# The last output row of a Strassen product made in two halves of 128 tokens

## The chip, the cores and the metric

The kernel runs on one core of one Trainium2 chip. The metric is device microseconds for one execution, the median of several. The profile is one execution taken by the hardware profiler; its own time stands beside its span below.

## The reference

One block of a streaming encoder on 512 tokens with 1024 channels: two parallel mixers (RWKV-7 and RG-LRU), cross-attention, a gated ConvFFN, and a last RMSNorm. What matters here is its end:

```python
def conv_ffn(h, w_in, conv_w, conv_b, w_out):
    u = h @ w_in
    gate = causal_dwconv(u[..., :D_FF], conv_w, conv_b)
    return (jax.nn.gelu(gate) * u[..., D_FF:]) @ w_out
...
x = x + conv_ffn(rms_norm(x, norm_ffn_g[l]), w_ffn_in[l], ffn_conv_w[l],
                 ffn_conv_b[l], w_ffn_out[l])
return rms_norm(x, norm_final_g)
```

`w_ffn_out` is 2816 x 1024. The last RMSNorm needs, for each token, the sum of squares over all 1024 channels, so no token can be stored before all its channels are there.

## The kernel before

Channels lie on the 128 partitions, in 8 blocks (`KB`), tokens along the free dimension (`T` = 512). The product with `w_ffn_out` is a Strassen product on a 2 x 2 split: channels out in two halves of 4 blocks (`MQ`), tokens in two halves of 256 (`H`, columns 0 to 255 and 256 to 511), the inner dimension in two halves of 11 blocks (`HB`). It takes seven products, called A11, A12, s1, s2, s3, A22 and s4 in that order, each 4 rows `m` of 11 weight blocks `k` of 128x128. Their sums build up in PSUM tiles, `X` (named ox_ps) and `YZ` (oyz_ps). The last product, s4, adds into `YZ[m][:, H:T]`, so when row m of it is done, tokens 256 to 511 of channel block m are final.

`out_product` (L1347) makes one product: for each (m, k) of `out_order` (L1313) it takes a weight tile from the stream `uf`, and `mm3` (L165 to L168) issues three matmuls, since a factor is kept as a high and a low part, both of type F32R (fp32r in the rows of ACT and DVE; the matmul rows write f32 for both types): high x high (L166), high x low (L167), low x high (L168). Each loads its own 128x128 weights (the PEld rows) and streams 256 columns. The weights come by `out_weights` (L1315): 8 tiles to a load on SP's queue, a cast on ACT (L1340) and a subtraction on DVE (L1341), three buffers deep.

When a row is done, `done(m)` is called. For s4 that is `c12` (L1422). It calls `ffn_out` (L1373): DVE adds the PSUM tile into the residual `xr` (L1380), ACT squares it (L1382), the block is scaled by the norm's weight (L1386 on ACT, or L1384 on DVE for the last row), and DVE adds the square to the running sum `sso` (L1388). For the last row, m = 3, `c12` goes over the two halves of 128 tokens, and for each calls `ffn_out` and then `final` (L1391):

- PE sums over the partitions with a matrix of ones: `sso` (L1394) and the last square (L1395), both plain F32 tiles, 128 columns to a half
- ACT takes Ln (L1406) and then twice Exp, once into PSUM for DVE (L1407) and once into SBUF for GpSimd (L1408)
- the 8 channel blocks are multiplied: two by GpSimd, twice three by DVE (all L1411), and stored as each is ready: DVE's first three from ACT's queue (L1415), the other two pieces from SP's queue (L1413)

Tokens 0 to 255 were normed and stored by `c21` after product A22, before this. The kernel is written with a Tile scheduler, which orders each engine's instructions by their place in the program unless a priority or an explicit order says otherwise, and puts in the waits between engines. `tc.issue_after` lets what is written inside follow a given instruction in the order.

Of the kernel before, what the change touches and what calls it, by code (L numbers as in the profile page):

```python
# [12 lines left out]
ALU = mybir.AluOpType  # L13
# [4 lines left out]
P = 128  # L18
T = 512
D = 1024  # L20
KB = D // P
# [37 lines left out]
def hybrid_block_kernel(ctx: ExitStack, tc: tile.TileContext, xT_d, mT_d, pv_d, cst_d, win_d, wk_d, wv_d,  # L59
# [18 lines left out]
    def rw_ps(name, pool=None, tag="rw", **kw):  # L78
        return (pool or prw).tile([P, T], F32, tag=tag, name=name, **kw)
# [9 lines left out]
    def par(name, i, n=1):  # L89
        o = PV[name][0]  # L90
        return pv[:, o + i:o + i + n]
# [45 lines left out]
    class Units:  # L137
# [10 lines left out]
        def next(self):  # L148
            if self.left == 0:
                self.fill()  # L150
            i = self.i
            self.i += 1
            self.left -= 1
            return self.hi[:, i * P:(i + 1) * P], self.lo[:, i * P:(i + 1) * P]
# [10 lines left out]
    def mm3(ps, lh, ll, rh, rl, start, stop, **kw):  # L165
        first = PE.matmul(ps, lh, rh, start=start, stop=False, **kw)  # L166
        PE.matmul(ps, lh, rl, start=False, stop=False, **kw)  # L167
        PE.matmul(ps, ll, rh, start=False, stop=stop, **kw)  # L168
        return first
# [3 lines left out]
    def sum_behind(ins, n=1):  # L173

        for put in islice(sums, n):
            tc.add_manual_dep(tc.keep_in_program_order(put()).ins, ins.ins.name, mybir.DependencyInfo(
                mybir.DependencyClass.Sync, mybir.DependencyReason.DATA), reason="pace of the sums")
# [44 lines left out]
    def rsqrt(out, src, scale, bias, load=True):  # L222

        if load:
            ins = ln_exp_set()
            with tc.issue_after(ins.ins):
                S.activation(out, src, AF.Ln, scale=scale, bias=bias)
                S.activation(out, out, AF.Exp, scale=-0.5)
        else:
            S.activation(out, src, AF.Ln, scale=scale, bias=bias)  # L230
            S.activation(out, out, AF.Exp, scale=-0.5)
# [51 lines left out]
    with tc.tile_pool(name="p0", bufs=1, reuse_waits="tile") as p0:  # L283
# [6 lines left out]
        o = PV["nmem"][0]  # L290
# [96 lines left out]
        for hf in range(2):  # L387
            pss = [(mm_ps if hf else rw_ps)(f"v_ps{hf}_{i}") for i in range(2)]
            for k2 in range(4):
                wh, wl = next(st)  # L390
# [105 lines left out]
    HB = FB // 2  # L496
    MQ = KB // 2
# [240 lines left out]
    with tc.tile_pool(name="pz", bufs=1, reuse_waits="tile") as pz:  # L738
# [9 lines left out]
        for s in range(30, -1, -1):  # L748
            n = 31 - s
# [25 lines left out]
    for i0 in (0, 16):  # L775
# [3 lines left out]
        for i in range(16):  # L779
            for e in range(2):  # L780
                r, k = rows[0][e], rows[1][e]
                PE.matmul(psh[e][k, i * 32:(i + 1) * 32], BZ[r, i0 + i, 32:64], ZA[r, i0 + i, :],
                          start=True, stop=True)
        for e, copy in enumerate((S.copy, V.tensor_copy)):
            k = rows[1][e]
            copy(Hs[e][k], psh[e][k].rearrange("p (i t) -> p i t", t=32))
        for i in range(16):
            for e in range(2):
                r, k = rows[0][e], rows[1][e]
                PE.matmul(pso[e][r, i * 32:(i + 1) * 32], Hs[e][k, i, :], BZ[k, i0 + i, 32:64],  # L790
                          start=True, stop=True)
# [357 lines left out]
    H = T // 2  # L1149
# [19 lines left out]
    for m in order:  # L1169
# [5 lines left out]
        i = m % 4  # L1175
# [17 lines left out]
        else:  # L1193
            sq = ph.tile([P, T], F32, tag="rsq", name=f"rsq_nffn{m}")
# [33 lines left out]
    gsets = [[pc.tile([P, n, 2, H], F32R, name=f"go0_{n}", bufs=1) for n in (8, 3)], [None, None], [None, None]]  # L1228
# [29 lines left out]
    for m0 in range(0, FB, NQ):  # L1258
        ms = range(m0, m0 + NQ)
        YZ = {m: pf.tile([P, T], F32, tag="yz", name=f"fyz_ps{m}", bufs=4) for m in ms}  # L1260
# [23 lines left out]
        for m in ms:  # L1284
# [10 lines left out]
            out = graw[:, m]  # L1295
            V.scalar_tensor_tensor(out[:, 0:H], X[m], -1.0, ac[:, 0:H], ALU.mult, ALU.mult)
            V.scalar_tensor_tensor(out[:, H:T], p5[m], -1.0, ac[:, H:T], ALU.mult, ALU.mult)
            k = m % HB
# [14 lines left out]
    out_order = [(m, k) for m in range(MQ) for k in range(HB)]  # L1313

    def out_weights():  # L1315

        flat = []
        for n in ("A11", "A12", "s1", "s2", "s3", "A22", "s4"):
            for m, k in out_order:
                if n[0] == "A":  # L1320
                    p, i = out_units(m, int(n[1]), int(n[2]))[k]
                    flat.append((p, wfo_d[p], i))
                else:
                    flat.append(((n, m), dO["s2" if n == "s4" else n, m], k))
        for g in range(0, len(flat), 8):
            units = flat[g:g + 8]
            n = len(units) * P
            with tc.high_priority():
                raw = wp.tile([P, 1024], F32, tag="wr", name=f"wfo_r{g // 8}", bufs=4)
                k = 0  # L1330
                while k < len(units):
                    key, src, i = units[k]
                    e = k
                    while e < len(units) and units[e][0] == key and units[e][2] == i + e - k:
                        e += 1
                    nc.sync.dma_start(raw[:, k * P:e * P], src[:, i * P:(i + e - k) * P])
                    k = e
                hi = wp.tile([P, 1024], F32R, tag="wh", name=f"wfo_h{g // 8}")
                lo = wp.tile([P, 1024], F32R, tag="wl", name=f"wfo_l{g // 8}")
                S.copy(hi[:, :n], raw[:, :n])  # L1340
                V.tensor_tensor(lo[:, :n], raw[:, :n], hi[:, :n].bitcast(F32), ALU.subtract)  # L1341
            for k in range(len(units)):
                yield hi[:, k * P:(k + 1) * P], lo[:, k * P:(k + 1) * P]

    uf = out_weights()

    def out_product(n, i, out, start, done, nsum=0):  # L1347

        for m, k in out_order:
            wh, wl = next(uf)  # L1350
            g = gsets[i][k // 8][:, k % 8]
            ins = mm3(out[m], wh, wl, g[:, 0, :], g[:, 1, :], start and k == 0, k == HB - 1,
                      skip_group_check=not start)
            if m * HB + k < nsum:
                sum_behind(ins)
            if k == HB - 1:
                done(m)

    def prepare(i, src):
        for k in K4:  # L1360
            split_g(i, src, k)
# [6 lines left out]
    YZ = [pf.tile([P, T], F32, tag="yz", name=f"oyz_ps{m}", bufs=4) for m in range(MQ)]  # L1368
    cols = (slice(0, H), slice(H, T))
# [3 lines left out]
    def ffn_out(src, snap, sign, m, ts, first=False, last=False):  # L1373

        n = ts.stop - ts.start
        if snap is not None:
            t1 = pc.tile([P, T], F32, tag="s", name=f"t1_{m}_{ts.start}")
            V.tensor_tensor(t1[:, :n], src, snap, ALU.add)
            src = t1[:, :n]
        V.tensor_tensor(xr[:, m, ts], xr[:, m, ts], src, sign)  # L1380
        sq = sso[:, ts] if first else pc.tile([P, T], F32, tag="ac", name=f"t2_{m}_{ts.start}")[:, :n]
        S.activation(sq, xr[:, m, ts], AF.Square)  # L1382
        if last:
            V.tensor_scalar(xr[:, m, ts], xr[:, m, ts], par("nfin", m), None, ALU.mult)  # L1384
        else:
            S.activation(xr[:, m, ts], xr[:, m, ts], AF.Identity, scale=par("nfin", m))  # L1386
        if not first and not last:
            V.tensor_tensor(sso[:, ts], sso[:, ts], sq, ALU.add)  # L1388
        return sq

    def final(ts, sq, nb, tag):  # L1391
        n = ts.stop - ts.start
        pss = rw_ps(f"rs_ps{ts.start}", pf, tag, bufs=4)
        PE.matmul(pss[:, :n], ones, sso[:, ts], start=True, stop=False)  # L1394
        PE.matmul(pss[:, :n], ones, sq, start=False, stop=True)  # L1395
        if nb < KB:
            rsqrt(ro[:, ts], pss[:, :n], 1.0 / D, eps[:, 0:1], load=False)
            for m in range(0, KB, nb):
                ms = slice(m, m + nb)
                V.tensor_tensor(xr[:, ms, ts], xr[:, ms, ts], ro[:, ts].unsqueeze(1).to_broadcast([P, nb, n]),  # L1400
                                ALU.mult)
                nc.sync.dma_start(out_d[:, ms, ts], xr[:, ms, ts])
            return

        rp = pf.tile([P, T], F32, tag="x", name=f"ro_ps{ts.start}", bufs=4)[:, :n]
        S.activation(ro[:, ts], pss[:, :n], AF.Ln, scale=1.0 / D, bias=eps[:, 0:1])  # L1406
        S.activation(rp, ro[:, ts], AF.Exp, scale=-0.5)  # L1407
        S.activation(ro[:, ts], ro[:, ts], AF.Exp, scale=-0.5)  # L1408
        for eng, r, m, w in ((nc.gpsimd, ro[:, ts], KB - NPOOL, NPOOL), (V, rp, 0, 3), (V, rp, 3, KB - NPOOL - 3)):
            ms = slice(m, m + w)  # L1410
            eng.tensor_tensor(xr[:, ms, ts], xr[:, ms, ts], r.unsqueeze(1).to_broadcast([P, w, n]), ALU.mult)  # L1411
            if m:
                nc.sync.dma_start(out_d[:, ms, ts], xr[:, ms, ts])  # L1413
            else:
                nc.scalar.dma_start(out_d[:, ms, ts], xr[:, ms, ts])  # L1415
# [3 lines left out]
        if m == MQ - 1:  # L1419
            final(cols[0], sq, 2, "x")  # L1420

    def c12(m):  # L1422
        if m < MQ - 1:
            ffn_out(YZ[m][:, H:T], None, ALU.add, m, cols[1])
        else:
            for o in (H, H + P):
                ts = slice(o, o + P)
                final(ts, ffn_out(YZ[m][:, ts], None, ALU.add, m, ts, last=True), KB, "yz")

    prepare(1, lambda ks: g2(ks, 1))  # L1430
    prepare(2, lambda ks: g1(ks, 1))
# [17 lines left out]
        split_g(0, lambda ks: g1(ks, 1), k)  # L1449
    out_product("s3", 2, X, False, lambda m: ffn_out(X[m], p5[m], ALU.subtract, MQ + m, cols[1], first=m == 0))  # L1450
    out_product("A22", 0, X, False, c21)
    out_product("s4", 1, [t[:, H:T] for t in YZ], False, c12)


# [75 lines left out]
```

## Time and profile before

| | us |
|---|---|
| median of 3 runs | 893.97 |
| lowest, highest | 891.78, 895.38 |
| the profiled execution | 894.56 |
| its span, first to last instruction | 892.8 |
| TensorE busy in it | 877.4 |

Times in the rows are microseconds from the span's start; mean durations of one instruction, where a row has them, are in nanoseconds. In the timeline rows a start is followed by a duration from that start to the end of the last of the merged instructions, the engine, the line, the operation, the tile written and the tile read, partitions x elements and the count; in brackets stands the idle time before, and who ended it. A matmul's row lasts longer than its slot, since matmuls are pipelined: the slot is read from one start to the next. A DMA's row on SPq or ACTq is the time that the queue's engine takes to issue it.

### The profile page before, as it was taken

To read this page: it belongs to the slowest core of one execution; us is meant where nothing else is said; L and a number is where in the kernel's file an instruction comes from. 1 tells how busy PE (TensorE), PEld (TensorE's weight loads), DVE (VectorE), ACT (ScalarE), POOL (GpSimd) and SP (SyncE) were. 2 spreads that over 40 slices of the span, in tenths; PEclk is the share of its full clock that TensorE was granted. 3 is DMA by queue.
4 is the path that set the end of the run, shared out by engine and by line. 5 is a ranking of instruction groups with operands and counts; after the bars stand their busy time and mean duration, and the time that the engine had idled before them with its cause. 6 is when DMAs were issued, how large, how long until landed. Compare 5 with 4: busy or idle time off the path is not lost.

```text
span 892.8 us, 15934 instructions
## 1 busy us (share of the span) xinstructions
PE 877.4 (98%) x6197; PEld 767.9 (86%) x6197; DVE 685.2 (77%) x1104; ACT 513.6 (58%) x783; POOL 132.5 (15%) x163
## 2 busy tenths in 40 slices
PE   8999999999999999999999999999999999999996
PEld 7878878888877677888888778999999999999996
DVE  6796598777967677675575578889888889999674
ACT  6575676634347676233554466766655656757563
POOL 0101222021102021001122111111111111211100
PEclk9999999999999999999999999999999999999999
DMA  7878899678997279758888958999999999998963
GB/s 268 307 253 215 206 228 233 187 203 233 262 227 156 72 203 249 220 166 229 218 234 183 197 137 185 260 275 271 265 255 294 263 297 275 244 276 220 261 202 94
DMA packets 97242, 201.37 MB, mean 226 GB/s; under 512 B 19536, under 2 KB 30928, under 8 KB 97104
## 3 DMA queue, kind: packets, MB, share of 16 engines
q1 hardware_dynamic: 62240, 118.57, 40.4%
q0 software_dynamic: 25504, 67.38, 36.9%
q10 hardware_dynamic: 9424, 14.42, 4.7%
q8 instruction: 48, 0.79, 0.4%
q14 instruction: 26, 0.21, 0.1%
HBM read 188.54 MB, written 78.12 MB: 299 GB/s over the span
## 4 chain that ended last, share of the span: by engine, by line
PE 91%; DVE 4%; DMA 2%; ACT 1%; issue 1%; DVEq 0%; ACTq 0%; SPq 0%
PE in_ps L167 7%; PE in_ps L166 7%; PE in_ps L168 7%; PE fx_ps L167 5%; PE fx_ps L166 5%; PE fx_ps L168 5%; PE fyz_ps L167 4%; PE fyz_ps L166 4%; PE fyz_ps L168 3%; PE ox_ps L166 2%; PE oyz_ps L166 2%; PE ox_ps L168 2%; PE oyz_ps L168 2%; PE oyz_ps L167 2%; PE ox_ps L167 2%; PE co_ps L167 2%
## 5 line engine op out<-in xcount | busy, mean ns | idle before, releaser
L132 ACT CAST wfi_h<-wfi_r 128x1024 fp32r<-128x1024 f32 x77 | 81.1, 1053 | 71.5 <-PE fx_ps L167 19.7
L168 PE MATMUL in_ps<-hT,win_l 128*128 128x512 f32 x304 | 121.3, 399 | 0.0
L167 PE MATMUL in_ps<-hT,win_h 128*128 128x512 f32 x304 | 121.0, 398 | 0.2 <-DVE hT L384 0.2
L166 PE MATMUL in_ps<-hT,win_h 128*128 128x512 f32 x304 | 120.6, 398 | 0.3 <-DVE pr L586 0.3
L133 DVE TENSOR_TENSOR wfi_l<-wfi_r,wfi_h 128x1024 fp32r<-128x1024 f32 x77 | 94.1, 1222 | 22.7 <-ACT wfi_h L132 22.4
L482 POOL DMA_DIRECT2D dS<-in_wfi x66 | 66.7, 1028 | 293.1 <-PE in_ps L166 102.3
L167 PEld LDWEIGHTS in_ps<-hT,win_h 128*128 128x128 f32 x304 | 57.1, 188 | 14.2 <-issue 0.7
L166 PEld LDWEIGHTS in_ps<-hT,win_h 128*128 128x128 f32 x304 | 57.1, 188 | 13.2 <-DVE pr L586 0.7
L168 PEld LDWEIGHTS in_ps<-hT,win_l 128*128 128x128 f32 x304 | 57.1, 188 | 13.1 <-issue 0.7
L518 POOL DMA_DIRECT2D dOs<-in_wfo x54 | 39.8, 784 | 181.5 <-PE fyz_ps L166 54.0
L118 DVE TENSOR_TENSOR win_l<-win_r,win_h 128x1024 fp32r<-128x1024 f32 x38 | 46.3, 1221 | 24.2 <-ACT win_h L117 20.7
L117 ACT CAST win_h<-win_r 128x1024 fp32r<-128x1024 f32 x38 | 39.9, 1050 | 41.1 <-PE in_ps L167 32.4
L1341 DVE TENSOR_TENSOR wfo_l<-wfo_r,wfo_h 128x1024 fp32r<-128x1024 f32 (+1 forms) x39 | 47.2, 1209 | 15.2 <-ACT wfo_h L1340 15.2
L1340 ACT CAST wfo_h<-wfo_r 128x1024 fp32r<-128x1024 f32 (+1 forms) x39 | 40.5, 1039 | 31.3 <-DMA wfo_r<-dOs 11.6
L168 PE MATMUL ox_ps<-go,wfo_l 128*128 128x256 f32 x176 | 49.1, 279 | 0.8 <-DVE wfo_l L1341 0.8
L166 PE MATMUL ox_ps<-go,wfo_h 128*128 128x256 f32 x176 | 49.2, 279 | 0.4 <-ACT wfo_h L1340 0.3
L166 PE MATMUL fx_ps<-hq,wfi_h 128*128 128x256 f32 x176 | 49.4, 280 | 0.0
L166 PE MATMUL fyz_ps<-hq,wfi_h 128*128 128x256 f32 x176 | 49.2, 280 | 0.0
L167 PE MATMUL fx_ps<-hq,wfi_h 128*128 128x256 f32 x176 | 49.2, 280 | 0.0
L167 PE MATMUL fyz_ps<-hq,wfi_h 128*128 128x256 f32 x176 | 49.2, 280 | 0.0
L167 PE MATMUL fx_ps<-hr,wfi_h 128*128 128x256 f32 x176 | 49.2, 280 | 0.0
L166 PE MATMUL fx_ps<-hr,wfi_h 128*128 128x256 f32 x176 | 49.2, 279 | 0.0
(432 smaller groups left out, 2704.9 us busy)
## 6 DMA issues: line engine op xcount, KB each, us to landing
dS<-in_wfi POOLq DMA_DIRECT2D x66, 512.0 KB, 7.8
wfi_r<-dS SPq DMA_DIRECT2D x44, 512.0 KB, 6.8
win_r<-in_win SPq DMA_DIRECT2D x38, 512.0 KB, 5.3
wfi_r<-in_wfi SPq DMA_DIRECT2D x33, 512.0 KB, 5.8
dS<-dS POOLq DMA_DIRECT2D x22, 512.0 KB, 5.7
dOs<-in_wfo POOLq DMA_DIRECT2D x12, 512.0 KB, 7.9
wk_r<-in_wk SPq DMA_DIRECT2D x8, 512.0 KB, 5.1
wv_r<-in_wv SPq DMA_DIRECT2D x8, 512.0 KB, 4.0
```

The costliest lines, as they stand in the source:

```text
L117: casts.append(S.copy(hi[:, o:o + n], raw[:, o:o + n]))
L118: V.tensor_tensor(lo[:, o:o + n], raw[:, o:o + n], hi[:, o:o + n].bitcast(F32), ALU.subtract)
L132: S.copy(hi, raw)
L133: V.tensor_tensor(lo, raw, hi.bitcast(F32), ALU.subtract)
L166: first = PE.matmul(ps, lh, rh, start=start, stop=False, **kw)
L167: PE.matmul(ps, lh, rl, start=False, stop=False, **kw)
L168: PE.matmul(ps, ll, rh, start=False, stop=stop, **kw)
L482: return lambda: nc.gpsimd.dma_start(s(out), src, **kw)
L518: yield lambda k=k, w=w, src=src: nc.gpsimd.dma_start(dO[n, m][:, k * P:(k + w) * P], src, **kw)
L1340: S.copy(hi[:, :n], raw[:, :n])
L1341: V.tensor_tensor(lo[:, :n], raw[:, :n], hi[:, :n].bitcast(F32), ALU.subtract)
```

## The change

The last product is made with `halves=True`. Rows 0 to 2 stay as they were. For row 3 the 11 weight tiles are taken from the stream first, and then the row is made twice, for tokens 256 to 383 and for 384 to 511, each with 11 x 3 matmuls of 128 columns into the half's columns of the same PSUM tile. After the first half its add, square and scaling are issued (`done(MQ - 1, 0)`); its `final` is issued behind the sixth weight block (k = 5) of the second half; the second half's follows at the end. `c12` is split to be called so.

```diff
-    def out_product(n, i, out, start, done, nsum=0):
-
-        for m, k in out_order:
+    def out_product(n, i, out, start, done, nsum=0, halves=False):
+
+        for m, k in out_order[:-HB] if halves else out_order:
...
+        if halves:
+
+            w = [next(uf) for _ in range(HB)]
+            for o in (0, P):
+                for k, (wh, wl) in enumerate(w):
+                    g = gsets[i][k // 8][:, k % 8, :, o:o + P]
+                    ins = mm3(out[MQ - 1][:, o:o + P], wh, wl, g[:, 0, :], g[:, 1, :], False, k == HB - 1,
+                              skip_group_check=True)
+                    if o and k == 5:
+                        with tc.issue_after(ins.ins):
+                            done(MQ - 1, 0, sq)
+                sq = done(MQ - 1, o)
+            done(MQ - 1, P, sq)
...
-    def c12(m):
-        if m < MQ - 1:
-            ffn_out(YZ[m][:, H:T], None, ALU.add, m, cols[1])
-        else:
-            for o in (H, H + P):
-                ts = slice(o, o + P)
-                final(ts, ffn_out(YZ[m][:, ts], None, ALU.add, m, ts, last=True), KB, "yz")
+    def c12(m, o=None, sq=None):
+        if o is None:
+            return ffn_out(YZ[m][:, H:T], None, ALU.add, m, cols[1])
+        ts = slice(H + o, H + o + P)
+        if sq is None:
+            return ffn_out(YZ[m][:, ts], None, ALU.add, m, ts, last=True)
+        final(ts, sq, KB, "yz")
...
-    out_product("s4", 1, [t[:, H:T] for t in YZ], False, c12)
+    out_product("s4", 1, [t[:, H:T] for t in YZ], False, c12, halves=True)
```

From here on the lines of the changed kernel stand 13 further down: L1380 is L1393 there, L1394 and L1395 are L1407 and L1408, L1411 is L1424.

The last rows of PE's queue before, from the last weight block of row 3 (oyz_ps_8128 is the PSUM tile of row 3, wfo_h and wfo_l the high and low weights, go the token factor, rs_ps the sum over partitions):

```order
L166 MATMUL oyz_ps_8128<-go_3_8115,wfo_h_9480 128x256
L167 MATMUL oyz_ps_8128<-go_3_8115,wfo_h_9480 128x256
L168 MATMUL oyz_ps_8128<-go_3_8115,wfo_l_9481 128x256
L1394 MATMUL rs_ps_9500<-sso,ones 128x128 [waits DVE_49]
L1394 MATMUL rs_ps_9517<-sso,ones 128x128
L1395 MATMUL rs_ps_9500<-t_3_256_9497,ones 128x128 [waits Activation_49]
L1395 MATMUL rs_ps_9517<-t_3_384_9514,ones 128x128 [waits Activation_49]
```

There the sums stand behind all products. PE's queue now, where the first half ends and the second begins:

```order
L166 MATMUL oyz_ps_8128<-go_3_8115,wfo_h_9459 128x128
L167 MATMUL oyz_ps_8128<-go_3_8115,wfo_h_9459 128x128
L168 MATMUL oyz_ps_8128<-go_3_8115,wfo_l_9460 128x128
L166 MATMUL oyz_ps_8128<-go_8_8114,wfo_h_9445 128x128 [waits DVE_49]
L167 MATMUL oyz_ps_8128<-go_8_8114,wfo_h_9445 128x128
L168 MATMUL oyz_ps_8128<-go_8_8114,wfo_l_9446 128x128
```

The matmuls are of 128 columns, and the first one of the second half waits for DVE. PE's queue at the sixth weight block of the second half:

```order
L166 MATMUL oyz_ps_8128<-go_8_8114,wfo_h_9445 128x128
L167 MATMUL oyz_ps_8128<-go_8_8114,wfo_h_9445 128x128
L168 MATMUL oyz_ps_8128<-go_8_8114,wfo_l_9446 128x128
L1407 MATMUL rs_ps_9518<-sso,ones 128x128
L1408 MATMUL rs_ps_9518<-t_3_256_9497,ones 128x128 [waits Activation_49]
L166 MATMUL oyz_ps_8128<-go_8_8114,wfo_h_9445 128x128
```

The first half's two sums now stand between the sixth and the seventh weight block of the second half; the other two stay at the end.

DVE's queue from the last `sso` add on, before (t the squares, ro_ps the norm's factor):

```order
L1388 TENSOR_TENSOR sso<-sso,t_2_256_9453 128x256 [waits Activation_49]
L1380 TENSOR_TENSOR xr<-xr,oyz_ps_8128 128x128 [waits PE_49]
L1380 TENSOR_TENSOR xr<-xr,oyz_ps_8128 128x128
L1384 TENSOR_SCALAR xr<-xr,pv 128x128 [waits Activation_49] x2
L1411 TENSOR_TENSOR xr<-xr,ro_ps_9503 128x3x128 [waits Activation_49]
L1411 TENSOR_TENSOR xr<-xr,ro_ps_9503 128x3x128 [waits DVE_49]
L1411 TENSOR_TENSOR xr<-xr,ro_ps_9520 128x3x128 [waits Activation_49]
L1411 TENSOR_TENSOR xr<-xr,ro_ps_9520 128x3x128 [waits DVE_49]
```

There the two halves alternate up to the multiplications. DVE's queue now:

```order
L1401 TENSOR_TENSOR sso<-sso,t_2_256_9453 128x256 [waits Activation_49]
L1393 TENSOR_TENSOR xr<-xr,oyz_ps_8128 128x128 [waits PE_49]
L1397 TENSOR_SCALAR xr<-xr,pv 128x128 [waits Activation_49]
L1424 TENSOR_TENSOR xr<-xr,ro_ps_9521 128x3x128 [waits Activation_49]
L1424 TENSOR_TENSOR xr<-xr,ro_ps_9521 128x3x128 [waits DVE_49]
L1393 TENSOR_TENSOR xr<-xr,oyz_ps_8128 128x128 [waits PE_49]
L1397 TENSOR_SCALAR xr<-xr,pv 128x128 [waits Activation_49]
L1424 TENSOR_TENSOR xr<-xr,ro_ps_9553 128x3x128 [waits Activation_49]
L1424 TENSOR_TENSOR xr<-xr,ro_ps_9553 128x3x128 [waits DVE_49]
```

The two halves no longer alternate: all of the first half's work stands ahead of the second half's add. ACT's queue has changed in the same way; the stores on SP's queue keep their order.

## Rows read from the trace of the kernel before

**Rows 1.** The page: span, busy time and instructions of PE, the chain by engine.
```profile
span 892.8 us, 15934 instructions
...
PE 877.4 (98%) x6197; PEld 767.9 (86%) x6197; DVE 685.2 (77%) x1104; ACT 513.6 (58%) x783; POOL 132.5 (15%) x163
...
PE 91%; DVE 4%; DMA 2%; ACT 1%; issue 1%; DVEq 0%; ACTq 0%; SPq 0%
```
**Rows 2.** Timeline of PE, 879.6 to 893 us: first and last of 33, then sums.
```profile
879.79 0.28 PE L166 MATMUL oyz_ps<-go,wfo_h 128*128 128x256 f32 x1
...
883.56 0.28 PE L168 MATMUL oyz_ps<-go,wfo_l 128*128 128x256 f32 x1
883.67 0.61 PE L1394 MATMUL rs_ps<-sso,ones 128*128 128x128 f32 x4
884.56 0.71 PE L1395 MATMUL rs_ps<-t,ones 128*128 128x128 f32 x4 [0.28 <-ACT t L1382]
```
**Rows 3.** Windows: length, busy time of each engine, granted clock, DMA share, GB/s.
```profile
880.00:884.00 4.00, 4.00 (x36) 4.00 (x35) 0.96 (x3) 0.93 (x2) 0.00 (x0) 1.00 0.00 0
```
**Rows 4.** The chain that ended last, 883.4 us on: start, us, what.
```profile
883.87 0.30 DVE xr L1380
...
884.19 0.32 ACT t L1382
...
884.56 0.50 PE rs_ps L1395 x2
...
885.08 0.63 ACT ro L1406 x2
```
**Rows 5.** Timelines of DVE, ACT, POOL and SP, 885 to 889.5 us.
```profile
885.60 0.48 ACT L1407 ACTIVATE ro_ps<-ro 128x128 f32<-128x128 f32 x2
...
885.91 1.95 DVE L1411 TENSOR_TENSOR xr<-xr,ro_ps 128x384 f32<-128x384 f32 x4 [0.89 <-ACT ro_ps L1407]
...
886.00 0.50 ACT L1408 ACTIVATE ro<-ro 128x128 f32<-128x128 f32 x2
...
886.44 0.72 POOL L1411 TENSOR_TENSOR xr<-xr,ro 128x256 f32<-128x256 f32 x1 [56.27 <-ACT ro L1408]
...
886.50 0.40 ACTq L1415 DMA_DIRECT2D out<-xr  x1
...
886.85 0.55 DVE L1411 TENSOR_TENSOR xr<-xr,ro_ps 128x384 f32<-128x384 f32 x1
...
887.19 0.37 SPq L1413 DMA_DIRECT2D out<-xr  x1
...
887.65 0.45 SPq L1413 DMA_DIRECT2D out<-xr  x1
...
888.75 0.69 SPq L1413 DMA_DIRECT2D out<-xr  x1
```
**Rows 6.** DMA from 886.5 to 892.8 us, in 40 slices: busy tenths, GB/s, sum.
```profile
DMA  0000008999999999999999999999930000000000
GB/s 0 0 0 0 0 20 260 296 263 280 270 296 263 309 302 293 289 254 299 293 276 250 322 299 283 277 289 296 283 98 0 0 0 0 0 0 0 0 0 0
DMA packets 2144, 1.05 MB, mean 167 GB/s; under 512 B 96, under 2 KB 2144, under 8 KB 2144
```
**Rows 7.** Line 1062, matmuls of one column: timeline; then durations (ns: min/median/max).
```profile
439.04 1.02 PE L1062 MATMUL rxc_ps<-ones,ssx 128*128 128x1 f32 x8
...
L1062 PE MATMUL rxc_ps<-ones,ssx x8: 242/250/250, 439.0 to 439.8; 128*128 128x1 f32 x8
```
**Rows 8.** Durations of lines 1394, 1406 and 919; line 919's timeline (256 columns, F32).
```profile
L1394 PE MATMUL rs_ps<-sso,ones x4: 272/275/275, 883.7 to 884.0; 128*128 128x128 f32 x4
...
L1406 ACT ACTIVATE ro<-rs_ps,eps x2: 360/364/367, 885.1 to 885.3; 128x128 f32<-128x128 f32 x2
...
328.07 1.02 PE L919 MATMUL gg<-sgx,gup 128*128 128x256 f32 x4
...
L919 PE MATMUL gg<-sgx,gup x16: 377/379/382, 328.1 to 346.0; 128*128 128x256 f32 x16
```

## The prediction

> **What bounds the kernel now.** I read the page first, then the end of the trace: the PE timeline, the chain of waits, the other engines' timelines, the DMA view. The page says that TensorE is busy 98% of the span and carries 91% of the chain that ended last [rows 1]. So what the change does on PE counts one for one, and what it does elsewhere counts only after PE's last product. Two stretches matter.
>
> The first is the last output row of the last product, 11 weight blocks with three matmuls each, 33 in all. In the PE timeline the first starts at 879.79 us and the last at 883.56 us, evenly: 3.77 us over 32 gaps is 0.1178 us each, so 33 cost 3.89 us [rows 2]. PE never waits there, and its granted clock is 1.00, the 2.4 GHz level [rows 3].
>
> The second is the tail, from the start of that last matmul (883.56) to the end of the span (892.8): 9.24 us. The chain shows its first part: add on DVE, square on ACT, sum over partitions on PE, Ln and Exp on ACT, multiplications on DVE, with the two halves of 128 tokens side by side at each step [rows 4]. So the second half's first multiplication starts at 886.85, one step pair behind the first half's 885.91 [rows 5]. Then come the stores. The first issue stands at 886.50 on ACT's queue, the last at 888.75 on SP's [rows 5]. In the DMA view (40 slices of 0.1575 us from 886.5) data flow without a break from the seventh slice (about 887.41) to the thirtieth (about 891.13): 1.05 MB in 3.7 us, 283 GB/s [rows 6]. The span ends 1.67 us after the last byte. The tail is thus bound by 2.35 us of chain (to 885.91), by 1.5 us until the first byte, and by 3.7 us of transfers.
>
> **The change part by part.**
>
> *Products by halves.* 33 matmuls of 256 columns (0.1178 us) become 66 of 128 columns, with the same weight tiles loaded again. Nothing in this trace multiplies two F32R tiles over fewer than 256 columns, so I bound the price of one.
> - From below: half of the 256-column price, 0.0589 us, if only columns count. 66 cost 3.89 us, no change.
> - A row speaks against that. The matmuls of line 1062 have one column and a 128x128 F32 weight tile; each is two records, each with its own weight load. Eight records take 1.02 us and one lasts 0.25, so (1.02 - 0.25)/7 = 0.110 us each [rows 7]. With one column nothing is left but the weight load. The 128-column sums of line 1394 come out nearly the same: (0.61 - 0.275)/3 = 0.112 us a record [rows 2, 8].
> - From above: an F32R matmul of 128 columns at the F32 price, two such records, 0.223 us.
>
> I take 0.112 us, since the F32R matmul is one record with one weight load of 128x128, as the records of lines 1062 and 1394 are. 66 x 0.112 = 7.39 us, against 3.89: **+3.50 us**, all of it on PE and so on the path. What hid the load before were 256 columns of streaming; 128 no longer cover it.
>
> By the Trainium skill's page "TensorE: Matmul & The Clock Gate", section "Back-to-back issue gap", a stream of weight loads and matmuls sustains about 81 ns at 128 columns. No run here shows that; 66 of them would cost 5.35 us, +1.46 us in place of +3.50, an estimate from that page.
>
> *A new wait on PE.* The built order gives the first matmul of the second half a wait on DVE that no product of this row had. Its value is that of the first half's add (line 1393), which reads the same PSUM tile. So PE stops until that add is done. The price from rows: the last product starts at 883.56, the add runs in the chain from 883.87 for 0.30 us, and PE picks up 0.05 us after what it waits for, as it does from the square's end (884.19 + 0.32) to 884.56 [rows 2, 4]. From the start of the last product to PE's next is 0.66 us where it was a slot of 0.112: **+0.55 us**. Bounds: zero, but the add can't be early, as it waits for that product; 0.66 us if none of the slot is hidden. Behind it in PE's queue stand all of the second half's products.
>
> The Trainium skill's page "PSUM — Partial Sum Buffer", section "PSUM bank collisions raise a hardware error", says that PE and another engine may not be in one bank at once. The two halves are columns of one tile, so by that rule the wait can't be dropped; without it the sum would be +2.0 us.
>
> *The first half's sum inside the stream.* Lines 1407 and 1408 now stand between the sixth and the seventh weight block of the second half: four records of 0.112 us [rows 2], **+0.45 us**. The square they need is ready 0.4 us after PE resumes, and 18 products (2.0 us) stand ahead of them: no wait. The second half's own line 1407 runs while DVE adds, as line 1394 did.
>
> *The tail after the last product, one half only.* Steps from the last product's start: add at +0.31, square +0.32, sum +0.37, Ln +0.52 [rows 4]; Exp once Ln is through (0.36 + 0.02 [rows 8], no second Ln between), first multiplication +0.31 (885.60 to 885.91 [rows 5]). That is 2.21 us. It ends 0.55 us later [rows 5]; ACT issues its store at 2.80, and data flow 0.91 us later, as from 886.50 to 887.41, at 3.71. SP's last store: the second Exp starts 0.20 behind the first (two in 0.48, 0.28 each), at 2.10, GpSimd 0.44 later, 0.72 us long, SP 0.03 after it and its second issue 0.46 later (887.19 to 887.65): 3.75, where it was 5.19. The second half's 0.52 MB need 1.85 us at 283 GB/s, to 5.56; with the same 1.67 us behind it the tail is 7.23 us against 9.24: **-2.0 us**. Bounds: -1.4 us if the last store takes its 4.05 us to the end as before, -2.2 us if its last transfer (0.20 MB, 0.69 us) alone sets the end: 3.75 + 0.91 + 0.69 + 1.67 = 7.02. This holds if the first half's data are gone by then. Its multiplications start at 887.48 (sum at 886.27, Ln 886.79, Exp 887.17), its store at 888.07, its data from 888.98 to 890.83; the second half's begin at 891.8.
>
> *DVE's queue.* The second half's add stands behind the first half's two multiplications. They start 0.467 us apart (four in 1.95 us, 0.55 each [rows 5]) and let DVE go at 888.40 to 888.49; the last product starts at 888.07, and its add wants 888.38. **+0.06 us**, here; this is what grows if PE is faster.
>
> Sum: 3.50 + 0.55 + 0.45 + 0.06 - 2.01 = **+2.6 us**. The profiled execution (894.56 us, span 892.8) would take 897.1; its time is 0.59 above the median of 893.97, so for the median I say **896.5 us**, +0.29%. With a pitch from 0.110 to 0.118 and the tail's bounds the sum lies between +2.2 and +3.6; this case's own range, with the spread of the runs, is 895.0 to 898.5.
>
> **Rivals.**
>
> *Narrow F32R products run at the F32 price* (the other side: clearly slower). Place: the 66 matmuls. If one costs two records, 0.223 us, 66 cost 14.7 us: +10.8 + 0.55 + 0.45 - 2.0 = +9.8, **903.8 us**. For it: 128-column work of that price is the only one in the trace [rows 2, 8], and no F32R product is narrower than 256. Against: the F32 matmul's extra record belongs to its type, since at 256 columns it also shows two records, of (1.02 - 0.379)/3 = 0.214 us each [rows 8], where F32R has one of 0.118. It decides from 0.142 us a product, where the sum passes +4.5 us.
>
> *Columns alone count.* At 0.0589 us PE pays nothing for the split. Then +0.60 for the wait (a shorter slot) + 0.45 - 2.0 = -0.95, but the second half's products end so early that the add waits some 0.8 us behind the multiplications: -0.15, **893.8 us**; 893.0 without that. For it: F32R at 512 and at 256 columns scales with columns. Against: the one-column row [rows 7]. The 81 ns of the skill's page lie between: by them about +0.9 us, 894.9, an estimate.
>
> *The halves don't overlap.* If the first half's stores left no earlier, only +4.5 us of PE would stay: 898.5. Against: nothing in the order holds the first half's chain back.
>
> **How the numbers follow.** About 0.5% (4.5 us) is what a measurement of this kernel tells from no change. The forecast has 0.62; the F32 price 0.26; columns alone, and prices up to the forecast's, 0.09; no overlap 0.03. Within 0.5%: forecast and columns, 0.70 with a little taken off for the spread. Slower: 0.28. Faster has 0.02: no case reaches -4.5 us; columns alone, the cheapest, ends near -1. Leaving the F32 price out would leave out over 2 in 10, so the range runs from columns alone to it: 892.8 to 904.2.
>
> **What would show it.** In the profile after: 66 matmuls of 128x128 on oyz_ps in about 7.4 us beside the sums; PE idle about 0.5 us before the second half's first one, released by DVE line 1393; four records of lines 1407 and 1408 in the stream; the first half's stores issued before the last product's end or within 0.5 us of it; DMA in two blocks of 1.8 us with a gap; a tail of about 7.2 us after the last product's start. A pitch of 0.06 or 0.22 makes the forecast wrong at its largest term; a last store that still takes 4 us to the end takes 0.6 us off the gain.

## The result, and the profile after

The changed kernel takes **896.07 us** (median of 20 runs, 892.16 to 898.40), the kernel before 893.69 us on the same chips (20 runs, 890.05 to 896.48). The ratio is 1.0026, with an interval of 1.0017 to 1.0035: 2.4 us slower (1.5 to 3.1). That is clear of the noise, though under the 0.5% that the forecast counts as a change. The forecast was +2.6 us and 896.5 us. The profiled execution took 896.71 us with a span of 894.9 us; 897.1 was forecast for it, which makes a span of 895.4. The page of the changed kernel, the rows that answer to [rows 1]:

```profile
span 894.9 us, 16001 instructions
...
PE 881.7 (99%) x6230; PEld 773.1 (86%) x6230; DVE 685.2 (77%) x1104; ACT 514.5 (57%) x783; POOL 132.6 (15%) x163
```

PE has 33 instructions more, as 33 products became 66, and is busy 4.3 us longer.

The timeline of PE in the changed kernel, 879.3 to 889.3 us, answers to [rows 2]. Shown are the first two and the last product of the first half, the first of the second half, the last ahead of the sums, the sums, the product behind them, the last product, and the second half's first sum:

```profile
879.40 0.22 PE L166 MATMUL oyz_ps<-go,wfo_h 128*128 128x128 f32 x1
879.46 0.28 PE L167 MATMUL oyz_ps<-go,wfo_h 128*128 128x128 f32 x1
...
882.92 0.27 PE L168 MATMUL oyz_ps<-go,wfo_l 128*128 128x128 f32 x1
883.58 0.33 PE L166 MATMUL oyz_ps<-go,wfo_h 128*128 128x128 f32 x1 [0.38 <-DVE xr L1393]
...
885.53 0.27 PE L168 MATMUL oyz_ps<-go,wfo_l 128*128 128x128 f32 x1
885.64 0.44 PE L1407 MATMUL rs_ps<-sso,ones 128*128 128x128 f32 x2
885.91 0.39 PE L1408 MATMUL rs_ps<-t,ones 128*128 128x128 f32 x2
886.05 0.31 PE L166 MATMUL oyz_ps<-go,wfo_h 128*128 128x128 f32 x1
...
887.65 0.28 PE L168 MATMUL oyz_ps<-go,wfo_l 128*128 128x128 f32 x1
887.76 0.43 PE L1407 MATMUL rs_ps<-sso,ones 128*128 128x128 f32 x2
```

From 879.40 to 882.92 are 32 gaps: 0.110 us each (0.06 the first, 0.112 the others), for half the columns of [rows 2], where a product took 0.1178. The whole row, from 879.40 to the end of the last slot at 887.76, takes 8.36 us, where it took 3.89. Of these the products take 7.40 us, the wait 0.55 (the last product's slot ends at 883.03, the next starts at 883.58) and the four records of sums 0.41 (885.64 to 886.05). The granted clock is 1.00 over this stretch, as in [rows 3]; the window of the changed kernel (columns as there):

```profile
879.40:887.70 8.30, 7.92 (x72) 7.78 (x70) 2.07 (x6) 2.20 (x6) 0.20 (x1) 1.00 0.01 2
```

The timeline of DVE in the changed kernel, 883 to 891 us, answers to [rows 4, 5]:

```profile
883.23 0.29 DVE L1393 TENSOR_TENSOR xr<-xr,oyz_ps 128x128 f32<-128x128 f32 x1 [2.30 <-PE oyz_ps L168]
...
887.05 1.02 DVE L1424 TENSOR_TENSOR xr<-xr,ro_ps 128x384 f32<-128x384 f32 x2 [2.87 <-ACT ro_ps L1420]
887.99 0.28 DVE L1393 TENSOR_TENSOR xr<-xr,oyz_ps 128x128 f32<-128x128 f32 x1
```

The first add starts 0.31 us after the first half's last product and holds PE until 883.58. The second add starts 0.34 us after the last product (887.65): it stands behind the two multiplications of the first half, and they let DVE go only 0.03 us late.

The first store on ACT's queue, the last on SP's, and the DMA view of the changed kernel from 886.5 to 894.9 us in 40 slices of 0.21 us, answer to [rows 5, 6]:

```profile
887.63 0.40 ACTq L1428 DMA_DIRECT2D out<-xr  x1
...
891.50 0.45 SPq L1426 DMA_DIRECT2D out<-xr  x1
```

```profile
DMA  0000000001999999996000059999999920000000
GB/s 0 0 0 0 0 0 0 0 0 29 285 261 307 283 246 307 290 295 190 2 0 0 0 149 280 295 293 241 317 285 300 268 68 0 0 0 0 0 0 0
```

The first half's first store is issued 0.02 us before the last product starts, and the data now go in two blocks with a gap of about 1 us between them. The second block begins at about 891.4 and ends at about 893.3; the span ends 1.6 us later. From the last product's start to the end of the span are 7.25 us, where it was 9.24.

So the stretch from the first matmul of the last row to the end of the span is 15.50 us long (879.40 to 894.9), where it was 13.01 (879.79 to 892.8): +2.49 us, as much as the medians differ. I call this the **end stretch**. It is the measure of the experiments beside their times, since it isn't touched by the few us by which profiled executions differ ahead of it (the last row begins between 876.2 and 882.4 us in them). It comes from one execution of each kernel.

### The profile page after: what moved, and what is told of

It is laid out like the page before. It is cut to its first block, busy times and chain, and to the rows that moved or that the text cites. A ratio compares the mean times of both kernels' runs of the same rounds, so it can differ in the third digit from the quotient of the medians.

```text
span 894.9 us, 16001 instructions
## 1 busy us (share of the span) xinstructions
PE 881.7 (99%) x6230; PEld 773.1 (86%) x6230; DVE 685.2 (77%) x1104; ACT 514.5 (57%) x783; POOL 132.6 (15%) x163
## 4 chain that ended last, share of the span: by engine, by line
PE 88%; DVE 6%; DMA 3%; ACT 1%; issue 1%; POOLq 0%; POOL 0%; SPq 0%; DVEq 0%
PE in_ps L167 6%; PE in_ps L168 6%; PE in_ps L166 6%; PE fx_ps L167 5%; PE fx_ps L166 5%; PE fx_ps L168 5%; PE fyz_ps L167 4%; PE fyz_ps L166 3%; PE fyz_ps L168 3%; PE ox_ps L167 2%; PE ox_ps L166 2%; PE ox_ps L168 2%; PE oyz_ps L167 2%; PE oyz_ps L166 2%; PE oyz_ps L168 2%; PE co_ps L167 2%
## 5 line engine op out<-in xcount | busy, mean ns | idle before, releaser
L166 PE MATMUL ox_ps<-go,wfo_h 128*128 128x256 f32 x176 | 49.2, 280 | 0.5 <-DVE graw L1296 0.5
L167 PE MATMUL ox_ps<-go,wfo_h 128*128 128x256 f32 x176 | 49.3, 280 | 0.0
L167 PE MATMUL fx_ps<-hr,wfi_h 128*128 128x256 f32 x176 | 49.3, 280 | 0.0
L168 PE MATMUL fx_ps<-hr,wfi_l 128*128 128x256 f32 x176 | 49.2, 279 | 0.0
```

## The experiments

The theory is that of the prediction: a product of 128 columns costs one load of its weights, 0.11 us; the seam costs 0.55 us; the sums 0.4; the tail gives 2.0 back, because the first half's stores are gone by then. The rivals are named in the expectations. In the diffs below a `+` stands for what the experiment has, and `...` for lines left out.

**The wait at the seam.** The second half gets a PSUM tile of its own, so that its first product need not wait for the first half's add. What was in that half of the shared tile is added to `xr` by one DVE instruction beforehand.

```diff
+            V.tensor_tensor(xr[:, MQ - 1, H + P:T], xr[:, MQ - 1, H + P:T], out[MQ - 1][:, P:H], ALU.add)
+            own = pf.tile([P, T], F32, tag="x", name="own", bufs=4)[:, 0:P]
-            for o in (0, P):
+            for o, dst in ((0, out[MQ - 1][:, 0:P]), (P, own)):
...
-                    ins = mm3(out[MQ - 1][:, o:o + P], wh, wl, g[:, 0, :], g[:, 1, :], False, k == HB - 1,
+                    ins = mm3(dst, wh, wl, g[:, 0, :], g[:, 1, :], o > 0 and k == 0, k == HB - 1,
...
```

> The second half's products of the last row go to a PSUM tile of their own (what that half of the old tile already holds is added into the residual by DVE before the row starts), so PE's wait on the first half's add is gone from the order. Theory (the wait costs 0.55 us of PE time on the path): the second half's first product follows the first half's last by 0.11 us instead of 0.66, everything behind it moves up by 0.55 us, and the kernel takes about 1.9 us more than the kernel before, where the change took 2.4. Rival (the wait is given back, since the second half's add then stands behind the first half's multiplications on DVE): the first half's chain would have to stay where it was, and the time would stay at +2.4 us.

Measured: 896.52 us (12 runs), ratio 1.0029 (1.0016 to 1.0042). The total can't tell it from the change, whose interval overlaps this one; the trace can. PE and DVE in this kernel, last product of the first half, first of the second, last of all, and the add behind it:

```profile
883.30 0.27 PE L168 MATMUL oyz_ps<-go,wfo_l 128*128 128x128 f32 x1
883.41 0.28 PE L166 MATMUL own<-go,wfo_h 128*128 128x128 f32 x1
...
887.43 0.28 PE L168 MATMUL own<-go,wfo_l 128*128 128x128 f32 x1
```

```profile
887.77 0.28 DVE L1395 TENSOR_TENSOR xr<-xr,own 128x128 f32<-128x128 f32 x1
```

The second half follows in the next slot, 0.11 us on, where it was 0.66. The add stands 0.34 us behind the last product, as before, so DVE does not take the gain back. The end stretch is 14.9 us (879.78 to 894.7): 0.6 less than the change's. In this trace the wait costs what the forecast said, and the rival that it would come back later falls.

**No overlap.** The first half's `final` is issued behind all of the second half's products.

```diff
-                    if o and k == 5:
-                        with tc.issue_after(ins.ins):
-                            done(MQ - 1, 0, sq)
+                if o:
+                    done(MQ - 1, 0, sq)
```

> The last row is still made by halves, but the first half's sum over partitions, its norm and its stores are issued behind the second half's products. Theory (the overlap is worth the difference of the tails): the products cost the same 7.3 us plus the wait of 0.55 us (in which PE now makes sums of the running total), so PE's last product ends 4.0 us later than before; the tail from the last product's start is about 8.7 us, since the 1.05 MB of both halves leave behind it, against 7.25 with the change and 9.24 before. In sum +3.5 us against the kernel before, about 1 us more than the change. Rival (the stores are hidden anyway and the overlap is worth nothing): the same +2.4 us as the change.

Measured: 896.82 us (12 runs), ratio 1.0030 (1.0019 to 1.0041), +2.7 us; an end stretch of 16.3 us (878.11 to 894.4), +0.8 over the change. PE's timeline at the seam of this kernel and its DMA view (884.4 to 894.4 us, slices of 0.25):

```profile
881.74 0.66 PE L1406 MATMUL rs_ps<-sso,ones 128*128 128x128 f32 x4
...
885.91 0.27 PE L168 MATMUL oyz_ps<-go,wfo_l 128*128 128x128 f32 x1
```

```profile
DMA  0000000000000000005999999999999992000000
```

The stores are one block again, and the tail is 8.5 us (885.91 to 894.4) against 7.25 in the change: the early norm and stores do shorten the end, by 1.2 us. The other 0.75 of the 2.0 us that the tail gives back is there without them (8.5 against 9.24): only one half's add and square stand behind the last product. Beside the change it loses only 0.8 of the 1.2, because no sums stand between the second half's products any more: those of `sso` come to stand at the seam and fill the wait, those of the square in the tail. The total lies below what was expected, with the interval (1.7 to 3.7 us) reaching to it.

**The place of the first half's norm.** `final` behind the tenth weight block in place of the sixth.

```diff
-                    if o and k == 5:
+                    if o and k == 9:
```

> The first half's sum and norm are issued behind the tenth weight block of the second half instead of the sixth, 12 products (1.33 us) later. Theory (DVE's queue: the second half's add stands behind the first half's two multiplications, which the change has just clear of it): those multiplications move 1.3 us later, the add is held by them and starts about 1.7 us after the last product's start instead of 0.34, and the time is about 1.35 us above the change's, +3.7 us against the kernel before. Rival (the place in PE's stream doesn't matter, as long as the first half's data leave before the second half's): the change's +2.4 us.

Measured: 898.0 us (8 runs), ratio 1.0044 (1.0028 to 1.0059), +3.85 us; an end stretch of 16.9 us (882.41 to 899.3), +1.4 over the change. PE and DVE in this kernel:

```profile
890.66 0.27 PE L168 MATMUL oyz_ps<-go,wfo_l 128*128 128x128 f32 x1
...
893.01 0.49 PE L1408 MATMUL rs_ps<-t,ones 128*128 128x128 f32 x2 [1.80 <-ACT t L1395]
```

```profile
891.40 1.02 DVE L1424 TENSOR_TENSOR xr<-xr,ro_ps 128x384 f32<-128x384 f32 x2 [4.21 <-ACT ro_ps L1420]
892.33 0.28 DVE L1393 TENSOR_TENSOR xr<-xr,oyz_ps 128x128 f32<-128x128 f32 x1
```

The second half's add starts 1.67 us after the last product, where it was 0.34: it stands in DVE's queue behind multiplications that themselves wait for ACT. This is the term of DVE's queue in the forecast (0.06 us), made large on purpose. PE's sum then waits 1.80 us for the square.

**The price of a narrow product, first look.** 192 and 64 tokens in place of 128 and 128.

```diff
-            for o in (0, P):
+            for o, n in ((0, 192), (192, 64)):
...
```

> The last row is split into 192 and 64 tokens instead of 128 and 128. Theory (a product under 256 columns costs one weight load, whatever its width): both parts' products start 0.110 us apart, 66 cost 7.3 us as in the change. Rival (two cycles a column at 2.4 GHz below 256 columns): 0.160 us for 192 columns and 0.053 for 64. The first part's sums in PE's stream cost 0.64 us instead of 0.45 (192 columns at the F32 rate), its multiplications hold DVE some 0.6 us past the second part's add, and the tail behind is about 1.5 us shorter than the change's (half the data, shorter steps): in sum some 0.7 us less than the change, +1.7 us against the kernel before.

Measured: 897.41 us (12 runs), ratio 1.0040 (1.0024 to 1.0055), +3.3 us, where +1.7 was expected: a miss. The end stretch is 15.45 us (878.05 to 893.5), not shorter than the change's. The timeline of PE in this kernel at the end of the first part, at the seam, and in the second part:

```profile
881.49 0.27 PE L167 MATMUL oyz_ps<-go,wfo_h 128*128 128x192 f32 x1
881.60 0.27 PE L168 MATMUL oyz_ps<-go,wfo_l 128*128 128x192 f32 x1
882.32 0.30 PE L166 MATMUL oyz_ps<-go,wfo_h 128*128 128x64 f32 x1 [0.45 <-DVE xr L1393]
...
886.46 0.28 PE L167 MATMUL oyz_ps<-go,wfo_h 128*128 128x64 f32 x1
886.57 0.28 PE L168 MATMUL oyz_ps<-go,wfo_l 128*128 128x64 f32 x1
```

On the question it was made for it is plain: 0.11 us a product with 192 columns and 0.11 with 64. A price that goes by columns falls. What I missed lies behind PE. DVE, SP's last store and DMA of this kernel (DMA from 883.5 to 893.5 us, slices of 0.25):

```profile
886.11 1.42 DVE L1424 TENSOR_TENSOR xr<-xr,ro_ps 128x576 f32<-128x576 f32 x2 [3.09 <-ACT ro_ps L1420]
887.45 0.21 DVE L1393 TENSOR_TENSOR xr<-xr,oyz_ps 128x64 f32<-128x64 f32 x1
...
890.36 0.44 SPq L1426 DMA_DIRECT2D out<-xr  x1
```

```profile
DMA  0000000000000000069999999995997592000000
GB/s 0 0 0 0 0 0 0 0 0 0 0 0 0 0 0 0 0 194 323 307 344 280 353 310 332 316 304 143 219 217 159 129 215 50 0 0 0 0 0 0
```

The larger first part keeps DVE for 1.42 us instead of 1.02, and the add starts 0.88 us after the last product; this hold was in the expectation (0.6 us). But the tail is 6.93 us, 0.3 shorter than the change's, where 0.9 was expected (1.5 less the 0.6). SP's last store is issued 3.79 us after the last product's start (890.36 - 886.57), in the change 3.85 (891.50 - 887.65): the hold has taken back what the shorter steps gave, and half the data do not end the span much sooner behind an issue that comes as late. The last 64 tokens, rows of 256 bytes, also go more slowly: where the DMA engines are nine tenths busy they run at 215 to 219 GB/s, the rows of 768 bytes ahead of them at 280 to 353. How the 0.6 us that are missing divide between the two isn't shown.

That small rows are slow to HBM is also what the Trainium skill says, page "DMA: Bandwidth & Descriptors", section "Why small descriptors are slow (HBM only)"; this trace agrees, with 215 to 219 GB/s against 280 to 353.

The median has a second part to it. Six of the 12 executions show a mean granted clock of 0.992 to 0.994, with a median of 899.3 us; the other six show 0.996 to 0.998, with 896.65, which is +2.5 us like the end stretch's +2.4. Of the 31 executions of the kernel before beside them one is under 0.995. No trace of one with the low clock was kept, so where it falls and why stays open.

**The price where it shows in the total.** To make it large, rows 0 to 2 of the last product are made by halves of 128 tokens in the kernel before, row 3 as it was; then by quarters of 64. Nothing else is changed: `done(m)` is called once a row.

```diff
-    def out_product(n, i, out, start, done, nsum=0):
+    def out_product(n, i, out, start, done, nsum=0, parts=0):
...
-        for m, k in out_order:
+        for m in range(MQ - 1 if parts else 0):
+            w = [next(uf) for _ in range(HB)]
+            for o in range(0, H, parts):
+                for k, (wh, wl) in enumerate(w):
+                    g = gsets[i][k // 8][:, k % 8, :, o:o + parts]
+                    mm3(out[m][:, o:o + parts], wh, wl, g[:, 0, :], g[:, 1, :], False, k == HB - 1,
+                        skip_group_check=True)
+            done(m)
+        for m, k in out_order[-HB:] if parts else out_order:
```

With 128:

> The kernel before, with rows 0 to 2 of the last product made by halves of 128 columns and the last row and the tail left as they were: the price of the split by itself, three times, with no wait and no early norm. Theory (each product costs one weight load, 0.110 us): 66 x 0.1105 - 3.89 = 3.4 us a row, +10.2 us for three. Rival (the wait and the sums in the stream make most of the change's cost on PE, the split products little): under 3 us.

Measured: 904.62 us (4 runs), ratio 1.0127 (1.0109 to 1.0146), **+11.1 us**. 198 products at 0.111 against 99 at 0.1178 make +10.3 us; the interval (9.7 to 13.0) holds it, and a price of two records (0.223, +32 us) is far outside it. Of the 0.8 us between, the trace shows 0.5 at the start of the product: PE waits for ACT before the sums of tokens 0 to 255, where the kernel before shows no wait. That row, and the windows of this kernel where nearly all of PE's work is such products:

```profile
868.46 0.70 PE L1403 MATMUL rs_ps<-t,ones 128*128 128x256 f32 x2 [0.51 <-ACT t L1390]
```

```profile
870.00:880.00 10.00, 10.00 (x92) 10.00 (x91) 4.48 (x7) 2.09 (x4) 0.00 (x0) 1.00 0.31 105
880.00:890.00 10.00, 10.00 (x92) 10.00 (x92) 2.67 (x4) 2.59 (x4) 0.00 (x0) 1.00 0.01 2
```

With 64:

> As the run with rows 0 to 2 by halves, but by quarters of 64 columns: 132 products a row. Theory (one weight load each, 0.110 us, whatever the width): 132 x 0.1105 - 3.89 = 10.7 us a row, +32 us for three. Rival (two cycles a column at 2.4 GHz below 256 columns, 0.055 us for 64): 132 x 0.055 - 3.89 = 3.4 us a row, +10 us, as by halves. A third: with a quarter of the columns the granted clock falls from its 2.4 GHz level in that stretch, and it costs more than 32 us.

Measured: 964.02 us (4 runs), ratio 1.0810 (1.0769 to 1.0851), **+70.5 us**: the case in which the clock falls, and a miss for the 32 us that I held to be likeliest. The windows of this kernel (the last column but two is the granted clock) and PE's timeline where it changes:

```profile
870.00:871.00 1.00, 1.00 (x12) 1.00 (x11) 0.38 (x1) 0.00 (x0) 0.00 (x0) 1.00 1.04 349
871.00:872.00 1.00, 1.00 (x8) 1.00 (x7) 0.00 (x0) 0.00 (x0) 0.00 (x0) 0.55 1.02 337
872.00:940.00 68.00, 68.00 (x320) 68.00 (x321) 4.05 (x6) 4.33 (x7) 0.00 (x0) 0.50 0.01 4
950.00:951.00 1.00, 1.00 (x11) 1.00 (x11) 0.00 (x0) 0.00 (x0) 0.00 (x0) 1.00 0.00 0
```

```profile
870.77 0.28 PE L166 MATMUL oyz_ps<-go,wfo_h 128*128 128x64 f32 x1
870.88 0.28 PE L167 MATMUL oyz_ps<-go,wfo_h 128*128 128x64 f32 x1
...
871.11 0.40 PE L166 MATMUL oyz_ps<-go,wfo_h 128*128 128x64 f32 x1
871.33 0.40 PE L167 MATMUL oyz_ps<-go,wfo_h 128*128 128x64 f32 x1
```

At the full clock 64 columns cost 0.11 us, as 128 and 192 do. Then the granted clock falls to 0.50, the level of 1.2 GHz, while PE is busy without a gap, and a product costs 0.213 us. Of the 396, 348 run so, from 871.11 to 945.35: 48 at 0.111 and 348 at 0.2133 are 79.6 us, where 99 at 0.1178 took 11.7. That is +68 us of the 70.5. Another 2 us are the first 19 products of 256 columns behind them, 4.2 us (945.35 to 949.55) instead of 2.2, until the clock is back.

**Fewer loads.** If loads are the price, a version with fewer of them should not pay it. Here the high weights meet both halves of the factor (its high and low part) in one matmul of 256 columns, and only the low weights make a narrow product: two loads a block and half instead of three. Each half has its own PSUM tile of 256 columns, whose two parts are added to `xr` one after the other (what was in the old tile is added beforehand), and the norm of the first half is issued behind the fourth block.

```diff
-                    ins = mm3(out[MQ - 1][:, o:o + P], wh, wl, g[:, 0, :], g[:, 1, :], False, k == HB - 1,
...
+                    ins = PE.matmul(own, wh, g, start=k == 0, stop=last)
+                    if not last:
+                        PE.matmul(own[:, 0:P], wl, g[:, 0, :], start=False, stop=False, skip_group_check=True)
-                    if o and k == 5:
+                    if o and k == 3:
...
+            V.tensor_tensor(xr[:, m, ts], xr[:, m, ts], own[:, P:H], ALU.add)
+            return ffn_out(own[:, 0:P], None, ALU.add, m, ts, last=True)
```

> The last row by halves, but for each half the high and the low part of the token factor go in one matmul of 2 x 128 columns against the high weights, into neighbouring columns of a PSUM tile of the half's own, beside one of 128 columns against the low weights; DVE adds both column blocks. What the old PSUM tile holds is added into the residual before the row. The first half's norm stands behind the fourth weight block of the second half. So 44 products replace 66, 22 of 256 and 22 of 128 columns. Theory (the price is the load of the weights, and 256 columns hide it): 22 x (0.118 + 0.111) = 5.0 us instead of 7.3, no wait on DVE at the half's end, one more add on the chain (0.2 us): from the row's first product to the end of the span about 12.9 us, where the kernel before takes 13.0 and the change 15.5; against the kernel before no difference that can be measured. Rival (a split costs by its restart, its extra sums and its tail, not by loads): at least 14.5 us, +1.5 us or more against the kernel before.

Measured: 893.49 us (12 runs) against 893.83 (16), ratio 0.9985 (0.9966 to 1.0003): no change against the kernel before, and faster than the changed kernel, whose interval lies above this one. PE's timeline of this kernel at the start of the row and at its last product, and the weight loads (PEld) of the first stretch:

```profile
876.38 0.33 PE L1369 MATMUL own<-go,wfo_h 128*128 128x256 f32 x1
876.55 0.22 PE L1371 MATMUL own<-go,wfo_l 128*128 128x128 f32 x1
876.61 0.33 PE L1369 MATMUL own<-go,wfo_h 128*128 128x256 f32 x1
...
881.73 0.34 PE L1369 MATMUL own<-go,wfo_h 128*128 128x256 f32 x1
```

```profile
876.44 0.19 PEld L1371 LDWEIGHTS own<-go,wfo_l 128*128 128x128 f32 x1
876.56 0.19 PEld L1369 LDWEIGHTS own<-go,wfo_h 128*128 128x128 f32 x1
876.66 0.19 PEld L1371 LDWEIGHTS own<-go,wfo_l 128*128 128x128 f32 x1
```

A pair takes 0.23 us (876.38 to 876.61), two loads, and 22 pairs 5.1 us instead of 7.40. A rival that no run was made for is a fixed price of any product, with or without the load. These rows speak against it: the loads start 0.10 to 0.12 us apart behind wide and narrow products alike, while the slots of the products are 0.17 and 0.06, so a product alone can take less than 0.11. The end stretch is 13.2 us (876.21 to 889.4) and its tail 7.67 us. So it removes 2.3 of the change's 2.5 us. The products make the 2.3, as the theory of loads has it; the wait, which is gone too (-0.55), is paid back by the tail (+0.4) and by the sums in the stream, which take 0.58 here. That its end stretch is 0.2 us longer than that of the kernel before says that the small gain of its median, if it is one, doesn't come from here. No version of this kind has much to win: with the products at their old price, 0.45 us for the sums against 2.0 us of tail would leave -1.5 us, 0.17%, an estimate from these rows.

## Why the prediction was right

| term | forecast, us | measured, us |
|---|---|---|
| 66 products for 33 | +3.50 | +3.51 (7.40 - 3.89) |
| wait of PE for the first add | +0.55 | +0.55; taken away, -0.6 |
| first half's sums in the stream | +0.45 | +0.41 |
| DVE's queue | +0.06 | +0.03; enlarged, +1.4 |
| tail | -2.01 | -2.02 (7.22 without the queue's 0.03) |
| sum | +2.6 | +2.5 (end stretch), +2.4 (medians) |

- **Products.** The row that decided was the one-column product of another line [rows 7]: 0.110 us for a bare load. F32R products of 64, 128 and 192 columns cost the same 0.11 us, and +11.1 us came out where 99 more of them ran. The weak place was that no row showed a narrow F32R product; the rival at the F32 price (0.223, 903.8 us) got 0.26 for that, and falls by the 0.110 us of the changed kernel. So does the rival that columns alone count (0.0589). The 81 ns at 128 columns of the Trainium skill's page "TensorE: Matmul & The Clock Gate", section "Back-to-back issue gap", appear in no run here: for these F32R weights the measured 110 ns decide, and the +0.9 us estimated from that page would have been too little. The Trainium skill's page "TensorE: Matmul & The Clock Gate", section "LDWEIGHTS (loading the stationary operand)", gives a load its number of columns divided by 1.2, in ns: 107 ns for 128, an estimate from that page. At the full clock these traces come near it, with 0.110 to 0.112 us; how a load goes with its columns is read from no run here, and at a granted clock of 0.50 the measured 0.213 decides.
- **The wait.** Its place and its size were right, and with a PSUM tile of its own the second half doesn't have it. That the two halves share a tile is thus the cause. It costs 0.55 us on PE and 0.6 in the end stretch; the medians don't show it.
- **The tail.** Two blocks of data with a gap came out as said, and the second begins 3.8 us after the last product, where 3.71 was worked out. The forecast gave the 2.0 us to the second half's data being alone. The run without overlap divides them: 1.2 us come from the early norm and stores, 0.75 from halving the row itself. With 192 tokens first, half the data behind the last product bought only 0.3 us of tail; the last store was issued as late as in the change.
- **No overlap** was mis-sized. I gave it 898.5 us by keeping wait, sums and the old tail. Tried alone it takes 896.8, for the sums of `sso` fill the wait and the tail is 8.5, not 9.24.
- **The chances.** 0.26 for the F32 price was much, given that the one-column row was there: the extra record of F32 products at 256 columns [rows 8] had already told that it belongs to the type.

Not settled: whether taking the wait away moves the median (its 0.6 us are within the interval), and why half the executions with 192 and 64 tokens ran at a lower granted clock.

## What to carry to other kernels

Before a product is cut into narrower pieces, look for the shortest matmul with a weight tile of the same size anywhere in the trace: it shows what the load alone costs, and no run of narrow pieces here got cheaper than that. Here 64, 128 and 192 columns cost the same 0.11 us, and 256 cost 0.118, so halves cost nearly twice as much, and the 2 us that the halves give back at the end don't pay for it; if pieces must be narrow, join what meets the same weights so that there are fewer loads. An overlap of this kind also has a seam (who reads the tile that the next piece writes) and a queue (whose work stands ahead of the last piece's first step), and both can be priced from rows of the kernel before.

## What the hardware showed that was not expected

- In the run with 64-column products the granted clock fell from 1.00 to 0.50 at about 871 us. PE had made such products from 864.94 on, with two records of sums among them, and from 866.5 on its row shows it busy without a gap. The clock was back at 1.00 by 950; PE had made 256-column products from 945.35 on. In the run with 128-column products it stands at 1.00 from 870 to 890. At the full clock 396 products at 0.111 against 99 at 0.1178 would have made +32 us; +70 were measured.
- At the lower level a 64-column product took 0.213 us, nearly twice its 0.11, and a 256-column one 0.213 as well: the price of a narrow product follows the granted clock, too.
- A 128-column product right behind one of 256 columns takes a slot of only 0.06 us (876.55 to 876.61; 879.40 to 879.46 in the changed kernel): its load had started beside the wide one (876.44). The wide one behind it then takes 0.17. Pairs come out at two loads, 0.23.
- In slices with the DMA engines nine tenths busy, stores with rows of 256 bytes ran at 215 to 219 GB/s, those with 512 bytes (the changed kernel) at 241 to 317.
